# Per-token reciprocal roots: turned into rows on TensorE before they are written to device memory

## The chip, the core and the metric

The kernel runs on one core of a Trainium2 chip. The core has TensorE (PE, matrix products; PEld is its loading of weights), VectorE (DVE), ScalarE (ACT), GpSimd (POOL) and SyncE (SP). Here SP issues all transfers, in the order of one queue; 16 DMA engines carry them out. The metric is the device time of one execution in microseconds (us).

## What is computed

Two layers of a mixer over 2048 tokens of width 1024, in float32. Cut to what matters here:

```python
def rms_norm(x, g):
    y = xf * lax.rsqrt(jnp.mean(xf * xf, axis=-1, keepdims=True) + EPS)
    return y * g

for l in range(DEPTH):
    shift, scale, gate = jnp.split(c_act @ w_ada[l] + b_ada[l], 3, axis=-1)
    h = rms_norm(x, norm_g[l]) * (1.0 + scale) + shift
    proj = h @ w_in[l]                       # nine parts: q, k, v, gates of two groups of heads
    y = concatenate([gla_branch(...), diff_branch(...)]) @ w_out[l]
    x = x + gate * y
```

The change touches the `rsqrt(mean(x*x) + EPS)` of `rms_norm`: one number per token, by which a whole column of the transposed input is multiplied.

## The kernel before

The tokens are cut into units of 512 (`UT`), four per layer, so there are eight units, counted from 0 in each layer, with keys 0 to 7 (`key = l * NU + u`). Activations lie transposed: features on the 128 partitions, tokens along the free dimension. A unit goes through preparation (`prep_gen`: the normalised input `hhi`, `hlo`), nine projections (`dense_gen`, `out_gen`: matmuls into `acc` banks), a linear-attention group (`gla_gen`) and four heads of softmax attention (`qk_gen`, `attn_gen`). Each float32 factor is split into a high and a low part (`hi`, `lo`; `oh`, `ol`), so a product takes three matmuls.

The weights `w` don't fit into the on-chip memory. They come once as `raw`, are split, and are written back to device memory (`wd`, L958); later units read them from there (`w<-wd`, L579 to L594) into four buffers (`p_w`, L389). Matmuls that wait for weights wait for these reads.

The reciprocal roots of a unit take the following way. Their sums of squares come from two places: in the first layer, units 1 to 3, from ScalarE (`prep_gen`: tiles `xt` of 128 tokens, squares with a running sum into `xss`); in the second layer, from the output of the layer before (`out_gen`: squares of `rt` are added into `sqs`, and four matmuls with `ones` sum over the partitions, `sum_squares`, L633). Either way there is a tile of 128 partitions x 4: token 128 t + p stands in partition p, column t. `root` (L639) scales it on VectorE (`xms`) and raises it to the power -1/2 on GpSimd (`xrs`). What the preparation needs is a row of 512 numbers, the same in all 128 partitions (`rsb`). So `rs_write` (L649) writes the tile to device memory in the order of the tokens (`rd`), and `prep_gen` reads it back, spread over all partitions (`rsb<-rd`). In that write neighbours in memory come from different partitions: it consists of 512 pieces of 4 bytes. Seven of the eight units take this way; unit 0 of the first layer (`start`) makes `rsb` with four matmuls.

The order of the work is not the order of the source. All instructions are recorded (`Program.record`, L148; so every line in the profile is L375, and tiles tell the groups apart), streams of the parts are interleaved by a rough clock of PE (`run_streams`), and a planner (`best_order`, L218, and `order`, L251) lays out the instructions of every engine by estimated costs, 60 times with small changes of priority chosen by a fixed random seed, and keeps the best layout. It takes into account dependences, buffers and PSUM banks. Each engine then runs its list strictly in that order. For a transfer it reckons with the bytes divided by a rate that depends on the length of the last dimension, 350 bytes per ns where it is neither 64 nor 256; so the write `rd` has the same cost to it in pieces of 4 and of 512 bytes.

Of the kernel before, what the change touches and what calls it, by code (L numbers as in the profile page):

```python
# [12 lines left out]
F32 = mybir.dt.float32  # L13
# [4 lines left out]
ALU = mybir.AluOpType  # L18
# [4 lines left out]
P = 128  # L23
# [3 lines left out]
TT = UT // P  # L27
# [351 lines left out]
def trunk_kernel(ctx, tc, xl, x, c, ccol, w_ada, w_mod, w_all, w_glr, w_gk, vecs, lam, out):  # L379
    nc = tc.nc  # L380
    L = w_all.shape[0]
    NU = xl.shape[0]
# [13 lines left out]
    cst = pool("cst", 1)  # L396
    p_t = pool("p_t", 3)
    p_sm = pool("p_sm", 4)
# [5 lines left out]
    V, A, G, T, SY = (prog.queue(e) for e in "VAGTS")  # L404
# [7 lines left out]
    def tp():  # L412
        return ps_t.tile([P, 512], F32, tag="tp", name="tp")
# [8 lines left out]
    ident = cst.tile([P, P], F32, name="ident")  # L422
# [5 lines left out]
    mhalf = cst.tile([P, 16], F32, name="mhalf")  # L428
# [99 lines left out]
    def done(*ev):  # L528
        events[ev] = clock[0]
# [103 lines left out]
    def sum_squares(sqs):  # L633
        ps = sc()
        for t in range(TT):
            T.matmul(ps[:, 2 * t:2 * t + 1], sqs[:, t * P:(t + 1) * P], ones[:, 0:1], start=True, stop=True)
        return ps[:, 0:2 * TT].rearrange("p (t o) -> p t o", o=2)[:, :, 0]

    def root(ss):  # L639
        ms = p_sm.tile([P, TT], F32, tag="xms", name="xms", bufs=2)  # L640
        V.tensor_scalar(ms, ss, 1.0 / D, EPS, op0=ALU.mult, op1=ALU.add)
        rs = p_sm.tile([P, TT], F32, tag="xrs", name="xrs", bufs=2)
        G.tensor_tensor(rs, ms, mhalf[:, 0:TT], op=ALU.pow)
        return rs

    def rs_tile():
        return p_x.tile([P, UT], F32, tag="rsb", name="rsb", bufs=2)

    def rs_write(key, rs):  # L649
        SY.dma_start(RD[key].rearrange("o (t p) -> p (o t)", p=P), rs)  # L650

    def prep_gen(l, u, xsrc):
        key = l * NU + u
        if l == 0:
            yield need("h", key - 1, lag=6.0)
            ss = p_sm.tile([P, TT], F32, tag="xss", name="xss", bufs=2)
            for t in range(TT):
                xt = p_q.tile([P, D], F32, tag="q", name="xt")
                SY.dma_start(xt, x[u * UT + t * P:u * UT + (t + 1) * P, :])
                A.activation(xt, xt, AF.Square, accum_out=ss[:, t:t + 1])  # L660
                yield pe(0, 2.0)
            rs_write(key, root(ss))
        rsb = rs_tile()
        SY.dma_start(rsb, RD[key].broadcast_to([P, UT]))
        yield need("free_h", key)
        yield need("ada", l, 1)
        alloc_h()
        for c in range(KT // 2):
            xp = p_q.tile([P, 2, UT], F32, tag="q", name="xp")
            SY.dma_start(xp, xsrc(u)[:, 2 * c:2 * c + 2, :])  # L670
            for j in range(2):
                make_h(l, 2 * c + j, xp[:, j, :], rsb)
            yield pe(0.44, 1.2)
        done("h", key)

    def start():
        y = layers[0]
        SY.dma_start(vec, vecs)
        SY.dma_start(cact, ccol)
        cb = p_s.tile([P, D], F32, tag="s", name="cb")  # L680
        SY.dma_start(cb, c.broadcast_to([P, D]))
        xs = []
        sqs = p_x.tile([P, UT], F32, tag="sqs", name="sqs")

        def mod_load(k):
            wm = p_s.tile([P, 2, D], F32, tag="s", name="wm")
            SY.dma_start(wm, w_mod[k])
            return wm

        for c_ in range(KT // 2):  # L690
            xp = p_q.tile([P, 2, UT], F32, tag="q", name="xp")
            SY.dma_start(xp, src_in(0)[:, 2 * c_:2 * c_ + 2, :])
            xs.append(xp)
        th = p_s.tile([P, D], F32, tag="s", name="th0")
        A.activation(th, cb, AF.Tanh, scale=0.5)
        V.scalar_tensor_tensor(cb, th, 1.0, cb, op0=ALU.add, op1=ALU.mult)
        t8 = p_sm.tile([P, KT], F32, tag="t8", name="t8", bufs=1)
        A.activation(t8, cact, AF.Tanh, scale=0.5)
        V.scalar_tensor_tensor(cact, t8, 1.0, cact, op0=ALU.add, op1=ALU.mult)
        V.tensor_scalar(cact, cact, 0.5, None, op0=ALU.mult)  # L700
        wm = [mod_load(0)]
        for it in FIRST:
            early[it, 0] = load_raw(0, it, 0)
        wm.append(mod_load(1))
        for k in range(KT):
            add_square(sqs, xs[k // 2][:, k % 2, :], k == 0)
        rs = root(sum_squares(sqs))
        dg = t2()
        pb = tp()
        for t in range(TT):  # L710
            ts_ = slice(t * P, (t + 1) * P)
            V.tensor_scalar(dg[:, ts_], ident, rs[:, t:t + 1], None, op0=ALU.mult)
            T.matmul(pb[:, ts_], ones, dg[:, ts_], start=True, stop=True)
        rsb = rs_tile()
        A.copy(rsb, pb)
        y.A = cst.tile([P, KT], F32, name="A0")
        y.B = cst.tile([P, KT], F32, name="B0")
        alloc_h()
        for k in range(KT):
            if k % 2 and k + 1 < KT:  # L720
                for it in FIRST:
                    early[it, (k + 1) // 2] = load_raw(0, it, k + 1)
            if k + 2 < KT:
                wm.append(mod_load(k + 2))
            sv = p_sm.tile([P, 2], F32, tag="sv", name="sv", bufs=2)
            for part in range(2):
                V.scalar_tensor_tensor(wm[k][:, part, :], wm[k][:, part, :], 0.5, cb, op0=ALU.mult, op1=ALU.mult,
                                       accum_out=sv[:, part:part + 1])
            V.tensor_tensor(y.B[:, k:k + 1], sv[:, 0:1], vec[:, R_B + k:R_B + k + 1], op=ALU.add)
            V.scalar_tensor_tensor(sv[:, 1:2], sv[:, 1:2], 1.0, vec[:, R_B + 8 + k:R_B + 9 + k], op0=ALU.add, op1=ALU.add)  # L730
            V.tensor_tensor(y.A[:, k:k + 1], sv[:, 1:2], vec[:, R_N + k:R_N + k + 1], op=ALU.mult)
            make_h(0, k, xs[k // 2][:, k % 2, :], rsb)
            for it, ring in zip(FIRST, (acc, sc)):
                hi, lo = weights(0, 0, it, k)
                if k == 0:
                    first_banks[it] = [ring() for _ in range(4)]
                for j in range(4):
                    (mm3T if it >= 4 else mm3N)(first_banks[it][j], k, slice(j * P, (j + 1) * P), hi, lo)
        gate_weights(0)
        done("ada", 0, 1)  # L740
        done("h", 0)
# [219 lines left out]
    RD = [dram.tile([1, UT], F32, name=f"rd{k}") for k in range(L * NU)]  # L961
# [262 lines left out]
    def out_gen(l, u):  # L1224
        y = layers[l]
        key = l * NU + u
        xsrc, xdst = io(l)
        final = key == L * NU - 1
        if u == NU - 1:
            yield need("attn", key, 3)  # L1230
        if l < L - 1:
            sqs = p_x.tile([P, UT], F32, tag="sqs", name="sqs")
        for hf in range(2):
            ds = slice(4 * hf, 4 * hf + 4)
            banks = []
            for n_, k in enumerate((4, 5, 6, 0, 1, 2, 3, 7)):
                yield need("oT", key, 0 if k < 4 else k, lag=0.8)
                if n_ == 4:
                    rt = p_o.tile([P, 4, UT], F32, tag="osb", name="rt")
                    SY.dma_start(rt, xsrc(u)[:, ds, :])  # L1240
                hi, lo = weights(l, u, 7 + hf, k)
                oh, ol = oTs[key, k]
                for j in range(4):
                    js = slice(j * P, (j + 1) * P)
                    if n_ == 0:
                        banks.append(acc())
                    T.matmul(banks[j], hi[:, js], oh, start=(n_ == 0), stop=False)
                    T.matmul(banks[j], hi[:, js], ol, start=False, stop=False)
                    T.matmul(banks[j], lo[:, js], oh, start=False, stop=(n_ == KT - 1))
                    yield pe(0.65)  # L1250
            yield need("ada", l, 2)
            xo = xdst(u)[:, ds, :]
            for j in range(4):
                d = 4 * hf + j
                V.scalar_tensor_tensor(rt[:, j, :], banks[j], y.gate[:, d:d + 1], rt[:, j, :], op0=ALU.mult, op1=ALU.add)
                if final and hf == 1:
                    SY.dma_start(xo[:, j, :], rt[:, j, :])
                elif j % 2:
                    SY.dma_start(xo[:, j - 1:j + 1, :], rt[:, j - 1:j + 1, :])
                if l < L - 1:  # L1260
                    add_square(sqs, rt[:, j, :], d == 0)
        if l < L - 1:
            rs_write(key + NU, root(sum_squares(sqs)))
        done("x", key)

    def chain(*gens):
# [113 lines left out]
```

## Time and profile before

| | |
|---|---|
| median of 3 runs | 2469.76 us (2467.94 to 2473.55) |
| profiled execution | 2479.16 us, span 2477.2 us |
| mean granted TensorE clock | 0.99 |
| PE busy | 2388.0 us, 96% of the span |
| DVE, ACT, POOL busy | 74%, 50%, 5% |
| DMA | 573.77 MB, mean 232 GB/s |

A profile is one execution. Its views used below are: the page with busy times and the chain of work that ended last; the list of waits (who waited for whom: us in total, times, longest); groups of instructions (busy us, mean ns of one, idle time before); the timeline (start, duration, engine, tiles, and in brackets the idle time of the engine before and what ended it); stretches (busy us of each engine, then granted clock, DMA share, GB/s); and DMA issues (tiles, count, KB each, median us from issue to landing). An x after a name counts instructions. A row of the timeline that ends in x2 or more merges neighbours, so its duration runs to the end of the last.

### The profile page before, as it was taken

The numbers are of one execution on the slowest core, as the hardware profiler recorded it, in microseconds if no ns is written. First come the engines' busy times: TensorE is split into PE (matmuls) and PEld (weight loads), VectorE is DVE, ScalarE is ACT, GpSimd is POOL, SyncE is SP. The second block draws the span as 40 slices with busy tenths as digits, with TensorE's granted clock in tenths as the row PEclk, the third lists the DMA queues.
The fourth block names the chain that finished last, engine by engine and source line by source line (L and its number), as shares of the span: only waits on it lengthen the run. The fifth ranks groups of instructions, "written<-read, shape, count | busy, mean of one in ns | idle before, by whom it ended". The sixth has DMA issues, their size and how long they took to land.

```text
span 2477.2 us, 38561 instructions
## 1 busy us (share of the span) xinstructions
PE 2388.0 (96%) x12896; PEld 1944.8 (79%) x12896; DVE 1827.2 (74%) x5158; ACT 1240.6 (50%) x2726; POOL 123.2 (5%) x400
## 2 busy tenths in 40 slices
PE   6899899999999999899999999999999999999998
PEld 5687587887788878787788777888788887888787
DVE  8878676896568877388975797568863888737983
ACT  4776543555245553255674576245633555425542
POOL 0010000000000000000000000000000000000000
PEclk9899899999999999999999999999999999999999
DMA  7567898786967769675757886765686767876663
GB/s 297 188 252 257 264 307 260 242 260 217 246 210 226 241 209 270 184 221 178 237 197 242 288 283 221 263 230 178 227 277 211 242 207 234 247 229 197 198 209 119
DMA packets 373165, 573.77 MB, mean 232 GB/s; under 512 B 195492, under 2 KB 255336, under 8 KB 369896
## 3 DMA queue, kind: packets, MB, share of 16 engines
q1 hardware_dynamic: 372968, 571.32, 71.6%
q8 instruction: 102, 1.67, 0.3%
q14 instruction: 95, 0.78, 0.1%
HBM read 416.03 MB, written 161.50 MB: 233 GB/s over the span
## 4 chain that ended last, share of the span: by engine, by line
PE 71%; DVE 15%; DMA 7%; ACT 4%; issue 2%; SPq 1%; POOL 0%; POOLq 0%; DVEq 0%; ACTq 0%
PE acc L375 47%; PE sc L375 11%; PE po L375 9%; DVE s L375 6%; PE tp L375 4%; DMA wr<-in_w_ada_dram 3%; DMA w<-wd 2%; DVE t L375 1%; DVE w L375 1%; DVE am L375 1%; ACT s L375 1%; SPq L375 1%; ACT qh L375 1%; DMA s<-ad 1%; DVE hlo L375 1%
## 5 line engine op out<-in xcount | busy, mean ns | idle before, releaser
L375 PE MATMUL acc<-w,hhi 128*128 128x512 f32 x2560 | 832.6, 401 | 9.5 <-DVE t L375 2.6
L375 PEld LDWEIGHTS acc<-w,hhi 128*128 128x128 f32 x2560 | 468.4, 190 | 100.2 <-DVE t L375 4.9
L375 PE MATMUL acc<-w,hlo 128*128 128x512 f32 x1280 | 506.7, 397 | 0.0
L375 ACT ACTIVATE s<-s,mx 128x512 f32<-128x512 f32 (+15 forms) x256 | 308.3, 1204 | 308.8 <-DVE s L375 162.7
L375 PE MATMUL acc<-oh,w 128*128 128x512 f32 x1024 | 358.7, 402 | 6.7 <-DMA w<-wd 3.6
L375 DVE TENSOR_SCALAR_CACHE_REDUCE s<-sc,mx 64x64 f32<-64x64 f32 (+5 forms) x640 | 307.6, 483 | 49.9 <-PE sc L375 29.8
L375 PE MATMUL acc<-hhi,w 128*128 128x512 f32 x960 | 323.4, 402 | 10.7 <-DMA w<-wd 9.5
L375 PEld LDWEIGHTS acc<-w,hlo 128*128 128x128 f32 x1280 | 242.2, 189 | 49.9 <-issue 0.9
L375 PEld LDWEIGHTS acc<-oh,w 128*128 128x128 f32 x1024 | 193.0, 189 | 50.3 <-DMA w<-wd 4.0
L375 PEld LDWEIGHTS acc<-hhi,w 128*128 128x128 f32 x960 | 181.5, 190 | 49.7 <-DMA w<-wd 11.1
L375 PEld LDWEIGHTS po<-Vj,s 128*128 128x128 f32 x1536 | 194.8, 197 | 11.1 <-DMA s<-ad 4.2
L375 PE MATMUL po<-Vj,s 128*128 128x128 f32 x1536 | 199.8, 282 | 3.5 <-DMA s<-ad 2.0
L375 PE MATMUL acc<-ol,w 128*128 128x512 f32 x512 | 202.2, 395 | 0.0
L375 DVE SCALAR_TENSOR_TENSOR s<-s,r 128x512 f32<-128x512 f32 (+2 forms) x320 | 198.5, 667 | 2.4
L375 PE MATMUL acc<-hlo,w 128*128 128x512 f32 x480 | 190.4, 397 | 0.0
L375 DVE TENSOR_SCALAR_CACHE_REDUCE s<-sc 128x512 f32<-128x512 f32 (+4 forms) x256 | 158.2, 622 | 41.4 <-PE sc L375 33.3
L375 PE MATMUL sc<-Kj,qh 128*128 128x512 f32 x384 | 162.0, 422 | 4.4 <-DVE s L375 4.4
L375 ACT CAST w<-raw 128x512 fp32r<-128x512 f32 x160 | 97.7, 622 | 112.1 <-PE acc L375 83.6
L375 PE MATMUL sc<-Kj,ql 128*128 128x512 f32 x384 | 152.2, 396 | 0.0
L375 DVE TENSOR_TENSOR w<-raw,w 128x512 fp32r<-128x512 f32 x160 | 108.9, 686 | 53.5 <-ACT w L375 52.7
L375 DVE SCALAR_TENSOR_TENSOR t<-ub,vec,t 128x512 f32<-128x512 f32 x192 | 138.3, 747 | 5.6 <-ACT t L375 5.1
L375 POOL MEMSET s<- 64x64 f32 x256 | 37.0, 145 | 2102.5 <-PE po L375 1522.7
(181 smaller groups left out, 3581.0 us busy)
## 6 DMA issues: line engine op xcount, KB each, us to landing
w<-wd SPq DMA_DIRECT2D x416, 512.0 KB, 4.5
wd<-w SPq DMA_DIRECT2D x144, 512.0 KB, 4.8
raw<-in_w_all_dram SPq DMA_DIRECT2D x80, 512.0 KB, 6.7
Kj<-kd SPq DMA_DIRECT2D x48, 512.0 KB, 5.5
ad<-s SPq DMA_DIRECT2D x24, 768.0 KB, 4.9
s<-ad SPq DMA_DIRECT2D x24, 768.0 KB, 6.7
wr<-in_w_ada_dram SPq DMA_DIRECT2D x128, 128.0 KB, 3.9
ad<-s SPq DMA_DIRECT2D x32, 512.0 KB, 4.1
```

Of the source, the lines that this page charges most:

```text
L375: getattr(self.engines[e], method)(*[real(a) for a in args], **{k: real(v) for k, v in kw.items()})
```

## The change

`root` now writes into the first four columns of a fixed tile of 128 x 128 (`rs128`, cleared once at the start). `rs_write` calls `root`, transposes the whole tile on PE into a PSUM bank, copies the first four rows to a tile `xrr` of 4 partitions x 128 on VectorE, and writes that: four rows of 128 consecutive tokens, so four pieces of 512 bytes. For unit 0 only the name of the tile changes.

```diff
+    rs128 = cst.tile([P, P], F32, name="rs128")
+    V.memset(rs128, 0.0)
+
     def root(ss):
         ms = p_sm.tile([P, TT], F32, tag="xms", name="xms", bufs=2)
         V.tensor_scalar(ms, ss, 1.0 / D, EPS, op0=ALU.mult, op1=ALU.add)
-        rs = p_sm.tile([P, TT], F32, tag="xrs", name="xrs", bufs=2)
-        G.tensor_tensor(rs, ms, mhalf[:, 0:TT], op=ALU.pow)
-        return rs
+        G.tensor_tensor(rs128[:, 0:TT], ms, mhalf[:, 0:TT], op=ALU.pow)
...
-    def rs_write(key, rs):
-        SY.dma_start(RD[key].rearrange("o (t p) -> p (o t)", p=P), rs)
+    def rs_write(key, ss):
+        root(ss)
+        ps = tp()
+        T.transpose(ps[:, 0:P], rs128, ident)
+        rr = p_sm.tile([TT, P], F32, tag="xrr", name="xrr", bufs=1)
+        V.tensor_copy(rr, ps[0:TT, 0:P])
+        SY.dma_start(RD[key].rearrange("o (t p) -> (o t) p", p=P), rr)
...
-            rs_write(key, root(ss))
+            rs_write(key, ss)
...
-        rs = root(sum_squares(sqs))
+        root(sum_squares(sqs))
...
-            V.tensor_scalar(dg[:, ts_], ident, rs[:, t:t + 1], None, op0=ALU.mult)
+            V.tensor_scalar(dg[:, ts_], ident, rs128[:, t:t + 1], None, op0=ALU.mult)
...
-            rs_write(key + NU, root(sum_squares(sqs)))
+            rs_write(key + NU, sum_squares(sqs))
```

PE has seven more instructions, VectorE eight; SP, ACT and POOL have as many as before. Since the planner lays out everything anew, neighbours change places all over the program. Three places matter below.

SP's queue at the roots of unit 3 of the first layer (in the trace near 587 us), before and now; `rd` is the write, `rsb<-rd` the read of it, `w<-wd` are weights, `vd`, `vp` and `Vj` values of the attention:

```order
L375 DMA Vj<-vp_1_1191 128x512
L375 DMA rd_6443<-xrs 128x4x1
L375 DMA vd_0_6497<-Vt 128x512
L375 DMA rsb<-rd_6443 128x512
L375 DMA w<-wd_7_1_3322 128x1024
L375 DMA w<-wd_7_2_3358 128x1024
L375 DMA vp_0_6543<-vd_0_6497 128x1x512
L375 DMA w<-wd_7_3_3448 128x1024
```

```order
L375 DMA Vj<-vp_1_1162 128x512
L375 DMA rd_6491<-xrr 4x128
L375 DMA vd_0_6510<-Vt 128x512
L375 DMA w<-wd_7_1_3324 128x1024
L375 DMA rsb<-rd_6491 128x512
L375 DMA w<-wd_7_2_3353 128x1024
L375 DMA vp_0_6556<-vd_0_6510 128x1x512
L375 DMA w<-wd_7_3_3427 128x1024
```

The write stands where it stood. One load of weights that stood behind the read `rsb<-rd` now stands ahead of it.

SP's queue at the roots of unit 2 of the second layer (near 988 us), before and now; `xd` is the residual stream, `ad` probabilities of the attention:

```order
L375 DMA s<-ad_3_10146 128x24x64
L375 DMA Vj<-vp_1_1191 128x512
L375 DMA rd_10223<-xrs 128x4x1
L375 DMA w<-wd_4_4_3985 128x1024
L375 DMA w<-wd_4_5_3992 128x1024
L375 DMA xd_9854<-rt 128x1024
L375 DMA w<-wd_4_6_4026 128x1024
L375 DMA Vj<-vp_1_4429 128x512
L375 DMA Vj<-vp_1_7504 128x512
L375 DMA w<-wd_4_7_4034 128x1024
```

```order
L375 DMA Vj<-vp_1_1162 128x512
L375 DMA w<-wd_4_4_3996 128x1024
L375 DMA rd_10249<-xrr 4x128
L375 DMA w<-wd_4_5_4018 128x1024
L375 DMA xd_9870<-rt 128x1024
L375 DMA w<-wd_4_6_4043 128x1024
L375 DMA Vj<-vp_1_4439 128x512
L375 DMA Vj<-vp_1_7520 128x512
L375 DMA w<-wd_4_7_4063 128x1024
```

One load of weights went from behind the write to ahead of it; three stand within the next six rows, as before.

PE's list at the same unit, from the sums of squares (`sc<-ones,sqs`) on, before and now:

```order
L375 MATMUL sc<-ones,sqs 128x1 x4
L375 MATMUL po<-Vt,s 128x128 x4
L375 MATMUL acc<-hhi,w 128x512
L375 MATMUL acc<-hlo,w 128x512
L375 MATMUL acc<-hhi,w 128x512 x2
L375 MATMUL acc<-hlo,w 128x512
L375 MATMUL acc<-hhi,w 128x512 x2
```

```order
L375 MATMUL sc<-ones,sqs 128x1 x4
L375 MATMUL po<-Vt,s 128x128 x4
L375 MATMUL acc<-hhi,w 128x512
L375 MATMUL acc<-hlo,w 128x512
L375 MATMUL acc<-hhi,w 128x512 x2
L375 MATMUL tp<-ident,rs_115 128x128
L375 MATMUL acc<-hlo,w 128x512
L375 MATMUL acc<-hhi,w 128x512 x2
```

The transpose stands eight matmuls behind the sums: four short ones of the attention (`po`) and four of the projection (`acc`).

## Prediction

> **What bounds the kernel now.** I read the page first: the engines' busy times and the chain that ended last.
>
> ```profile
> span 2477.2 us, 38561 instructions
> ...
> PE 2388.0 (96%) x12896; PEld 1944.8 (79%) x12896; DVE 1827.2 (74%) x5158; ACT 1240.6 (50%) x2726; POOL 123.2 (5%) x400
> ...
> PE 71%; DVE 15%; DMA 7%; ACT 4%; issue 2%; SPq 1%; POOL 0%; POOLq 0%; DVEq 0%; ACTq 0%
> ```
>
> TensorE (PE) is busy for 2388.0 of 2477.2 us. A change that takes no matmul away can therefore win only out of the 89.2 us in which PE idles, and out of stretches in which its granted clock is below full. So the next view is who PE waited for, and the one after it is PE's timeline at the longest of these waits.
>
> ```profile
> PE acc L375 <- DMA w<-wd: 15.5, 5, 6.2
> PE sc L375 <- DVE sqs L375: 14.7, 1, 14.7
> ```
>
> ```profile
> 385.98 0.70 PE L375 MATMUL acc<-w,hhi 128*128 128x512 f32 x2 [2.40 <-DMA w<-wd]
> 603.00 0.50 PE L375 MATMUL acc<-oh,w 128*128 128x512 f32 x1 [3.58 <-DMA w<-wd]
> 674.09 0.50 PE L375 MATMUL acc<-hhi,w 128*128 128x512 f32 x1 [2.95 <-DMA w<-wd]
> 1001.01 0.80 PE L375 MATMUL acc<-hhi,w 128*128 128x512 f32 x1 [6.22 <-DMA w<-wd]
> ```
>
> The wait for `sqs` is the start of the program and stays. The largest other item is the wait for weights `w` read back from device memory: 15.5 us, of which these four make 2.40 + 3.58 + 2.95 + 6.22 = 15.15. What stood in the DMA queue ahead of each? The timeline of SyncE (SP), the only queue that issues transfers, answers:
>
> ```profile
> 363.61 1.36 SPq L375 DMA_DIRECT2D rd<-xrs  x1
> ...
> 586.85 0.37 SPq L375 DMA_DIRECT2D rd<-xrs  x1
> 590.38 0.32 SPq L375 DMA_DIRECT2D vd<-Vt  x1
> 595.68 0.32 SPq L375 DMA_DIRECT2D rsb<-rd  x1
> 596.10 0.86 SPq L375 DMA_DIRECT2D w<-wd  x2
> ...
> 659.74 0.37 SPq L375 DMA_DIRECT2D rd<-xrs  x1
> ...
> 988.06 0.39 SPq L375 DMA_DIRECT2D rd<-xrs  x1
> 988.54 0.93 SPq L375 DMA_DIRECT2D w<-wd  x2
> ```
>
> Each of the four waits ends 13 to 22 us after a write `rd<-xrs`, which is the write that the change rewrites. The DMA issues tell how odd this write is: it has 2 KB and lands later than 512 KB of weights.
>
> ```profile
> w<-wd SPq DMA_DIRECT2D x416, 512.0 KB, 4.5
> ...
> wd<-w SPq DMA_DIRECT2D x144, 512.0 KB, 4.8
> ...
> wr<-in_w_ada_dram SPq DMA_DIRECT2D x128, 128.0 KB, 3.9
> ...
> rd<-xrs SPq DMA_DIRECT2D x7, 2.0 KB, 11.5
> ```
>
> Last I read stretches of 6 to 8 us behind four of the writes, and a normal stretch of the same kind. The last three columns are granted clock, busy share of the DMA engines, and GB/s.
>
> ```profile
> 368.00:374.00 6.00, 5.18 (x23) 3.98 (x23) 1.39 (x2) 1.24 (x2) 0.00 (x0) 1.00 1.25 114
> 662.00:670.00 8.00, 8.00 (x38) 6.58 (x38) 1.10 (x2) 1.35 (x4) 0.69 (x2) 1.00 1.08 72
> 990.00:998.00 8.00, 4.79 (x33) 4.10 (x31) 0.35 (x1) 0.66 (x3) 0.69 (x2) 1.00 1.14 57
> 1358.00:1366.00 8.00, 8.00 (x37) 6.61 (x36) 1.37 (x2) 1.25 (x2) 0.00 (x0) 1.00 1.13 99
> 1366.00:1374.00 8.00, 8.00 (x38) 6.42 (x36) 5.37 (x12) 5.79 (x10) 0.00 (x0) 1.00 0.97 364
> ```
>
> Behind a write of 512 pieces the DMA engines are shown as fully busy, and they move 57 to 114 GB/s instead of 364. The large transfers issued next crawl for some 8 us. That is the mechanism on which the prediction rests.
>
> **The change part by part.** *The write itself.* The two weight loads to look at are the one issued at 988.54 and the one at 664.56; asked for singly, they show
>
> ```profile
> w<-wd SPq DMA_DIRECT2D x1, 512.0 KB, 12.4
> ```
>
> ```profile
> w<-wd SPq DMA_DIRECT2D x1, 512.0 KB, 9.5
> ```
>
> 988.54 + 12.4 is 1000.9 and 664.56 + 9.5 is 674.1: the moments at which PE starts again. With the usual 4.5 they would be there at 993.0 and 669.1. PE stopped at 1001.01 − 6.22 = 994.8 and 674.09 − 2.95 = 671.1, so both waits go. At 603.00 the way is another one: the read `rsb<-rd` has to wait until the write has landed, and holds SP from 590.7 to 595.68 with the weight loads behind it. PE stopped at 599.4. In the new order one weight load stands ahead of that read; it leaves at about 590.8 and is there at 595.3. At 385.98 it was SP that came late. Its waits between 370 and 381 are led by
>
> ```profile
> SPq L375 <- DMA wr<-in_w_ada_dram: 5.5, 1, 5.5
> ```
>
> a load of 128 KB that fell into the stretch of 114 GB/s; with it SP was held 5.5 us, more than PE's 2.40. So 15.15 us of waiting can go.
>
> *The clock.* Behind three of these waits the granted clock fell:
>
> ```profile
> 602.00:608.00 6.00, 5.00 (x15) 3.96 (x16) 2.84 (x6) 0.00 (x0) 0.00 (x0) 0.72 0.88 356
> 674.00:680.00 6.00, 5.59 (x16) 4.20 (x17) 0.00 (x0) 0.00 (x0) 0.00 (x0) 0.72 0.40 162
> 1001.00:1007.00 6.00, 5.99 (x15) 4.58 (x16) 0.75 (x1) 0.69 (x1) 0.00 (x0) 0.52 0.84 339
> ```
>
> 6 us at 0.72 lose 1.7 us of PE's work, twice, and 6 us at 0.52 lose 2.9: together 6.3 us. The gain is at most 15.15 + 6.3 = 21.4 us.
>
> *What comes back at once.* Where the weights no longer end the wait, the vector engines may. Behind 990 VectorE (DVE) is busy 0.35 and ScalarE (ACT) 0.66 of 8 us, behind 662 DVE 1.10: both have time to spare. Behind 586 they haven't:
>
> ```profile
> 588.00:596.00 8.00, 8.00 (x39) 6.39 (x38) 6.45 (x26) 2.84 (x11) 0.15 (x1) 1.00 0.13 38
> ```
>
> DVE is busy 6.45 of 8 us there. I count this place as given back whole, 3.58 + 1.7 = 5.3 us, so 16.1 us remain. That is my choice; it may be 0.
>
> *What is added.* On PE seven transposes, on DVE seven copies out of PSUM and one fill at the start. The nearest rows:
>
> ```profile
> L375 PE MATMUL tp<-ident,rw 128*128 128x128 f32 x256 | 42.9, 276 | 3.2 <-DVE rw L375 3.0
> ...
> L375 DVE COPY a_sb<-tp 128x8 f32<-128x8 f32 x16 | 1.9, 157 | 1.6 <-PE tp L375 1.6
> ```
>
> A transpose takes 276 ns alone and 42.9 / 256 = 0.17 us among others, so 1.2 to 1.9 us on the engine that sets the end; I take 1.9, since each stands alone. The copies, 7 x 157 ns = 1.1 us, lie beside matmuls, as DVE has a quarter of the span free; uncovered they would cost that 1.1.
>
> *The new wait.* PE runs its queue in order. Now a transpose stands in it that needs the root from GpSimd (POOL), and behind it stand the matmuls of the projections. How long the root takes shows at 657:
>
> ```profile
> 657.84 0.58 PE L375 MATMUL sc<-ones,sqs 128*128 128x1 f32 x4
> 658.46 0.16 DVE L375 TENSOR_SCALAR xms<-sc 128x4 f32<-128x4 f32 x1
> 658.71 1.01 POOL L375 TENSOR_TENSOR xrs<-xms,mhalf 128x4 f32<-128x4 f32 x1 [0.55 <-DVE xms L375]
> ```
>
> From the end of the sums on PE (658.42) to the end of the root (659.72) it is 1.30 us. In the new order eight matmuls lie between at the unit quoted in the section on the change, four of 8.00 / 38 = 0.21 us (the stretch from 662) and four short ones. I take the short ones at the 0.17 of a transpose: 1.5 us in all. The root is just hidden. At the four places of this kind I take 0.15 us each, 0.6 in all. At the other three the root hangs on ACT's squares of the loaded `xt`:
>
> ```profile
> 108.94 0.17 DVE L375 TENSOR_SCALAR xms<-xss 128x4 f32<-128x4 f32 x1 [0.62 <-ACT xt L375]
> ...
> ACT s L375 <- DVE s L375: 163.2, 102, 8.4
> ```
>
> DVE waited 0.62 us for those there; I take 0.6 for PE each time, 1.8 in all. The far bound is the longest single wait of ACT for DVE, 8.4 us each. Below nothing the wait can't be. SP now waits for the copy instead of the root, some 0.8 us later (0.276 + 0.157 and hand-offs); behind it stand weight loads. At 988.54 these have 994.8 − 993.0 = 1.8 us to spare, so it costs nothing there; without that cover it would cost the 0.8.
>
> *The order.* The planner redraws the order of the whole program, and on PE it differs in many small places. I take 0 for it, and a bound of 3 us either way: that is a fifth of the 15.5 us which the longest group of waits in the trace makes.
>
> *The sum.* −21.4 + 5.3 + 1.9 + 0.6 + 1.8 = −11.8 us. The profiled execution took 2479.16 us, of which its span is 2477.2; the median of the runs is 2469.76, 9.4 us less. I subtract the sum from both: 2467.4 for a profiled execution, and **2458 us** for the median. That the unprofiled runs have the same waits is an assumption.
>
> *A rule and the rows.* The new write is not in the trace. Its nearest rows are the load of 128 KB, 3.9 us, and the old write, 11.5 us. I take the lower, as it has 4 pieces and the old one 512; with the upper one and the crawl behind it the sum would be the first rival's. The Trainium skill, page "DMA: Bandwidth & Descriptors", section "Specifications", names 512 bytes as the least size of a transfer at full rate, below which the DMA engine reads, changes and writes back. By this rule the new write just escapes, and the sum is the −11.8 above. The trace agrees that 4 bytes are far too little (11.5 us for 2 KB), and no run here shows where the border lies.
>
> **The rivals.** *First: the pieces are not what is slow.* It could be the write into device memory itself, or what else runs in those moments. Then the landing stays at 11.5, the queue crawls as before, the four waits stay, and only the costs come: 1.9 + 0.6 + 1.8 = 4.3 us at most, 2474, nearer to 2472 if the holds stay hidden. In this case the change does not do what it says. For it speaks that only runs with such writes are at hand. Against it speak four slow stretches behind four such writes, while weight writes to the same memory land in 4.8 us. The Trainium skill gives this rival a ground: on the same page, section "Anatomy of one DMA — SWDGE (gpsimd) path", it says of another way of issuing that a transfer's fixed cost is mostly the receipt of the write, and "This can cause a surprisingly long delay especially when the write target is HBM." The trace shows long landings of this write, and not which of the two it is.
>
> *Second: the waits go, and PE finds the next one.* PE may meet attention's vector work earlier at more places than 603. If two thirds of the 21.4 come back, the sum is −7.1 + 4.3 = −2.8, 2467. For it: DVE 74% busy and 15% of the chain. Against it: DVE and ACT stand nearly idle behind 662 and 990.
>
> *Third, slower: PE is held at the transposes of the first layer.* In the three units whose root hangs on ACT, PE reaches the transpose with the root not there. Everything behind it waits, projections included. With the bound of 8.4 us each and a half-clock stretch of 1.7 behind each, this is 3 x 10.1 = 30.3 us against 16.1 − 1.9 − 0.6 = 13.6 of gain: 16.7 us slower, 2486. It decides for slower by over 0.2% from a hold of 13.6 + 4.9 = 18.5 us in all. Against it: ACT is busy for half the span only, and DVE waited just 0.62 us there.
>
> **How the numbers follow.** 0.2% is 4.9 us, about what a measurement of this kernel can tell from no change; so faster means under 2464.8 and slower over 2474.7. The forecast has 0.68 (0.63 faster, 0.05 same), its own range 2446 to 2466: the low end is −21.4 + 1.2 − 3 = −23.2 us. The first rival has 0.10 (0.07 same, 0.03 slower), the second 0.14 (0.07 faster, 0.06 same, 0.01 slower), the third 0.08 (0.01 same, 0.07 slower). Together: faster 0.70, same 0.19, slower 0.11. The range runs from 2446 to 2473 and takes in most of the first two rivals.
>
> **What would show it.** Right: `rd` lands within about 4 us, the stretches behind it move over 300 GB/s, PE's waits for `w` fall from 15.5 us to under 5, and no half-clock stretch stands near 603, 674 and 1001. The holds show as PE's waits at `tp<-ident,rs`, 2.4 us in all. Wrong: `rd` still lands after 8 us or more; or waits for `w` are gone while PE's idle time is as long, now ended by DVE or ACT; or single holds at the transposes of over 5 us.

## The result and the profile after

| | before | after |
|---|---|---|
| median | 2469.02 us (4 runs) | 2447.16 us (4 runs, 2444.97 to 2448.36) |
| profiled execution | 2479.16 us, span 2477.2 | 2444.97 us, span 2443.3 |

The ratio is 0.9907, with a 95% interval of 0.989 to 0.9924: faster by 21.9 us. The forecast was −11.8 us, so the direction was right and the size short by nearly half. The two profiles lie further apart than the medians (34.2 us), because the profiled execution of before was 9.4 us above its median; a second profile of it, below, took 2467.67 us.

The page of the changed kernel, its span, busy times and chain:

```profile
span 2443.3 us, 38591 instructions
...
PE 2375.5 (97%) x12903; PEld 1941.1 (79%) x12903; DVE 1828.8 (75%) x5166; ACT 1240.2 (51%) x2726; POOL 124.3 (5%) x400
...
PE 75%; DVE 13%; DMA 5%; ACT 4%; issue 2%; POOL 0%; SPq 0%; POOLq 0%; DVEq 0%; ACTq 0%
```

PE idles for 67.8 us instead of 89.2, and its busy time is 12.5 us shorter in spite of seven more matmuls (8.5 us against the second profile of before, 2384.0): fewer of them ran at a reduced clock. The list of waits shows what became of the 15.5 us:

```profile
PE sc L375 <- DVE sqs L375: 14.6, 1, 14.6
PE sc L375 <- DVE s L375: 8.7, 10, 1.7
...
PE acc L375 <- DMA w<-wd: 0.3, 1, 0.3
```

PE's waiting for weights has gone, and no DMA stands among its larger waits. Had the write itself become fast? Its landing is not recorded in this trace, but the read of it tells. It waits for the write to land, and the timeline of SP's queue at the first unit shows when it leaves:

```profile
111.68 0.27 SPq L375 DMA_DIRECT2D rd<-xrr  x1
...
113.31 0.38 SPq L375 DMA_DIRECT2D rsb<-rd  x1
```

Write and read lie 1.63 us apart, so the write landed within that time; before, a write took 11.5 us to land. The stretches behind three of the writes (357.0, 644.9 and 967.4 us); the last columns are clock, DMA share and GB/s:

```profile
361.00:367.00 6.00, 6.00 (x32) 5.06 (x31) 2.14 (x5) 2.17 (x6) 0.69 (x2) 1.00 0.93 374
648.00:656.00 8.00, 8.00 (x39) 6.60 (x38) 0.75 (x1) 0.69 (x1) 0.00 (x0) 1.00 0.39 137
970.00:978.00 8.00, 8.00 (x49) 7.07 (x48) 0.35 (x1) 1.35 (x4) 0.69 (x2) 1.00 0.99 355
```

Where much is asked of the DMA engines they move 355 to 374 GB/s; the 137 stands beside a share of 0.39, so little was asked there. Before, shares of 1.08 to 1.25 went with 57 to 114. PE is busy without a gap in all three. Last, the group of what was added, and the idle time of the engines ahead of its instructions:

```profile
L375 PE MATMUL tp<-ident,rs x7: 270/272/473, 110.6 to 1327.9; 128*128 128x128 f32 x7
...
  POOL rs L375: 0.7, 3
```

A transpose takes 272 ns (minimum, median and maximum stand before the times), and an engine of the group waited for the root three times, 0.7 us in all. PE's matmuls are not among them: twice it was the weight loading of a transpose (PEld), 0.4 us in all, and once DVE at unit 0, which waited as long in the kernel before.

### The profile page after: what moved, and what is told of

It reads as the page before. It is cut to its first block, busy times and chain, and to the rows that moved or that the text cites. A ratio compares the mean times of both kernels' runs of the same rounds, so it can differ in the third digit from the quotient of the medians.

```text
span 2443.3 us, 38591 instructions
## 1 busy us (share of the span) xinstructions
PE 2375.5 (97%) x12903; PEld 1941.1 (79%) x12903; DVE 1828.8 (75%) x5166; ACT 1240.2 (51%) x2726; POOL 124.3 (5%) x400
## 4 chain that ended last, share of the span: by engine, by line
PE 75%; DVE 13%; DMA 5%; ACT 4%; issue 2%; POOL 0%; SPq 0%; POOLq 0%; DVEq 0%; ACTq 0%
PE acc L375 50%; PE sc L375 11%; PE po L375 9%; DVE s L375 6%; PE tp L375 4%; DMA wr<-in_w_ada_dram 2%; DVE t L375 1%; ACT s L375 1%; DVE w L375 1%; DMA xt<-in_x_dram 1%; ACT qh L375 1%; DVE am L375 0%; ACT t L375 0%; DVE r L375 0%; DMA xp<-xd 0%
```

## The experiments

The theory: 512 pieces of 4 bytes keep the DMA engines busy for some 10 us, and what is queued behind the write crawls, whoever waits for it. The first rival: the late landing of the write is what costs (its reader holds SP). The second: it is the new order of the program that pays. In all kernels an edit is put in where the recorded instructions are issued, behind the planner, unless it is said otherwise, so that it moves nothing else. A ratio is taken to executions of the kernel before that belong to the same series; their median was 2469.02 us in one series and 2471.24 in another, so times of different series can be compared to some 2 us only.

**The kernel before, once more** (`e0_before_again`, nothing edited).

> The kernel before, unchanged, for a second profile of it. The pieces theory (512 pieces of 4 bytes clog the DMA queue for some 8 us and the weight loads behind them come late) expects the same picture: PE waits for w of 10 to 16 us, all within 25 us of a write rd, and time 2465 to 2474 us. If the four waits of the first profile were an accident of that execution, their sum is under 5 us here.

Measured: 2467.79 us, ratio 0.9991 (0.9979 to 1.0004). PE's waits for weights in this second profile, the group and the single ones:

```profile
PE acc L375 <- DMA w<-wd: 10.7, 5, 5.4
```

```profile
384.55 0.70 PE L375 MATMUL acc<-w,hhi 128*128 128x512 f32 x2 [1.19 <-DMA w<-wd]
598.85 0.50 PE L375 MATMUL acc<-oh,w 128*128 128x512 f32 x1 [2.66 <-DMA w<-wd]
668.22 0.50 PE L375 MATMUL acc<-hhi,w 128*128 128x512 f32 x1 [1.24 <-DMA w<-wd]
...
992.55 0.79 PE L375 MATMUL acc<-hhi,w 128*128 128x512 f32 x1 [5.38 <-DMA w<-wd]
```

The places are the four of the prediction, so they belong to the kernel. Their sizes do not: 15.5 us in the first profile, 10.7 in this one.

**The new order with the old pieces** (`e1_after_order_512`). Transposes and copies stay, in their places; the write takes the column tile again, in 512 pieces.

```diff
+            args = self.swap.get(i, args)
...
+        prog.swap[len(prog.ops)] = (RD[key].rearrange("o (t p) -> p (o t)", p=P), rs128[:, 0:TT])
         SY.dma_start(RD[key].rearrange("o (t p) -> (o t) p", p=P), rr)
```

> The changed kernel in its own order of instructions, transposes and copies included; only the write goes out of the root's tile again in 512 pieces of 4 bytes. Pieces theory: the gain goes, 2462 to 2474 us, PE waits for w again 8 us or more. Order theory (the new layout of the program is what gained): the gain stays, 2445 to 2452 us, no waits for w.

Measured: 2464.48 us, ratio 0.997 (0.9958 to 0.9982).

```profile
PE acc L377 <- DMA w<-wd: 7.3, 4, 2.6
```

With the old pieces two thirds of the gain are lost, and PE's waits for weights are back, at 7.3 us a little under the 8 expected. The order is worth something of its own, some 7 us with the costs of the transposes in it. The wait near 600 us is missing here: the weight load that the new order put ahead of the read leaves at 586.56 us, while the read is held until 589.94; in the second profile of before the read left at 591.67 and that load behind it. Whether this explains the 7 us was not tried by itself.

**The old order with the new write** (`e2_before_order_turned`). Before, with each write replaced, where it stands, by transpose, copy and a write of four pieces.

```diff
+        def turned(eng, dst, src):
+            ps = ps_t.pool.tile([P, 512], F32, tag="tp", name="tp")
+            eng["T"].transpose(ps[0:TT, 0:P], src, ident.real())
+            rr = p_sm.pool.tile([TT, P], F32, tag="xrr", name="xrr", bufs=1)
+            eng["V"].tensor_copy(rr, ps[0:TT, 0:P])
+            eng["S"].dma_start(RD[key].real().rearrange("o (t p) -> (o t) p", p=P), rr)
+        prog.turn[len(prog.ops)] = turned
```

> The order of the kernel before, kept for all its instructions; each write rd is replaced, where it stands, by a transpose, a copy and a write in 4 pieces of 512 bytes. Pieces theory: 2444 to 2454 us, no waits for w near the writes. Order theory: 2462 to 2474 us.

Measured: 2449.56 us, ratio 0.991 (0.9896 to 0.9923), PE's waits for weights 0.3 us. The write alone makes the whole gain; the second rival falls. The two effects do not add: the order pays 7 us only while the old pieces are there.

The two kernels of the same order can be laid side by side. Below are four stretches of before (second profile) that begin near a write, and then the stretches of this experiment with the same matmuls:

```profile
279.20:366.40 87.20, 83.08 (x402) 67.28 (x402) 63.33 (x171) 42.93 (x94) 4.18 (x11) 0.98 0.90 309
584.50:668.20 83.70, 79.82 (x401) 65.98 (x399) 52.29 (x143) 30.03 (x66) 5.19 (x14) 0.98 0.82 234
963.60:1052.90 89.30, 83.92 (x402) 69.71 (x401) 39.90 (x98) 26.02 (x57) 2.76 (x8) 0.96 0.71 204
1334.80:1484.50 149.70, 145.94 (x802) 116.10 (x801) 117.82 (x330) 87.00 (x205) 7.24 (x23) 1.00 0.81 275
```

```profile
282.20:363.90 81.70, 80.82 (x403) 66.14 (x403) 63.98 (x171) 42.68 (x93) 4.17 (x11) 1.00 0.92 323
582.00:659.70 77.70, 77.70 (x402) 65.16 (x401) 52.47 (x144) 29.65 (x63) 4.76 (x13) 1.00 0.79 252
954.50:1035.80 81.30, 81.30 (x403) 67.77 (x402) 40.48 (x100) 26.03 (x57) 3.08 (x8) 1.00 0.69 223
1317.60:1463.60 146.00, 144.71 (x803) 116.28 (x802) 118.15 (x331) 87.32 (x205) 7.24 (x23) 1.00 0.79 282
```

The second number of a row is its length: 5.5, 6.0, 8.0 and 3.7 us shorter, 23.2 in all, more than the 16.4 by which the two spans differ. The clock is enough for the rest. Read in stretches of 5 us, one minus the granted clock adds up to 6.8 us in before within these four stretches and to nothing in the experiment, but elsewhere to 13.6 us in before and 22.2 in the experiment. Those other losses lie before 130 us, near 260 and, in the experiment, near 2410; they differ from one execution to the next. Two of the places, the first and the last, hardly show among the waits for `w`. At the first, the waits of DVE and PE between 282 and 306 us of before say why:

```profile
DVE am L375 <- DMA wr<-in_w_ada_dram: 11.1, 4, 5.7
...
PE tp L375 <- DVE rw L375: 2.4, 1, 2.4
...
PE acc L375 <- DVE z L375: 0.9, 1, 0.9
```

and in the same part of the experiment

```profile
DVE am L379 <- DMA wr<-in_w_ada_dram: 3.9, 2, 3.2
```

Other loads, of 128 KB, crawl too. DVE stands before them 11.1 us instead of 3.9, what is queued behind on DVE comes late, and PE's wait appears under the name of DVE. PE's two lines have no counterpart in the experiment. At the last place ACT waits 7.4 us for transfers `wd<-w` in before and 0.6 us in the experiment.

**One old write kept** (`e7_key3_old`): the experiment before, with the 512 pieces left at unit 3 of the first layer, the place near 600 us.

```diff
-        prog.turn[len(prog.ops)] = turned
+        if key != 3:
+            prog.turn[len(prog.ops)] = turned
```

> The order of the kernel before with the transposed write at six of the seven places; at unit 3 of the first layer (the wait that ended at 603 us) the old write in 512 pieces stays. The prediction counted this place as given back whole to VectorE: then this is as fast as with all seven, 2447 to 2452 us. If nothing is given back there, it is slower by the wait and the half clock behind it, 4 to 6 us: 2453 to 2457 us.

Measured: 2452.96 us, ratio 0.9925 (0.9901 to 0.9948), 3.4 us more than with all seven turned, at the lower edge of the 4 to 6 us expected. The two intervals overlap, so the time alone does not decide; the trace carries the verdict:

```profile
595.55 0.50 PE L379 MATMUL acc<-oh,w 128*128 128x512 f32 x1 [2.32 <-DMA w<-wd]
```

```profile
585.00:593.00 8.00, 8.00 (x40) 6.40 (x38) 5.36 (x19) 3.06 (x5) 0.00 (x0) 1.00 0.38 64
```

The wait is back where the old write is. With all seven turned PE is busy 79.39 of the 80 us from 560 on, here 77.29: the 2.1 us that go with the wait are not taken back by DVE or ACT. The half clock did not come with it: from 596 to 602 us the granted clock is 1.00.

**A write that nobody reads** (`e3_unread_512x4`). The changed kernel, plus behind each write a second one of 512 pieces of 4 bytes, into memory that nothing reads; no instruction waits for it.

```diff
+        def again(eng):
+            extra = dram.pool.tile([1, UT], F32, name=f"rx{key}")
+            r = rs128.real()
+            eng["S"].dma_start(extra.rearrange("o (t p) -> p (o t)", p=P), r[:, 0:TT])
+        prog.more[len(prog.ops)] = again
```

> The changed kernel, and behind each of its seven writes one more write of the same 2 KB in 512 pieces of 4 bytes to memory that nobody reads and nobody waits for. Pieces theory: the queue clogs as before, 2458 to 2474 us, PE waits for w of 8 us or more. Landing theory (what cost time was that the read of the roots had to wait for a late landing): 2445 to 2451 us, as nothing waits for this write.

Measured: 2472.06 us, ratio 0.9998 (0.9987 to 1.001). The waits, and two stretches behind such writes:

```profile
PE acc L376 <- DMA w<-wd: 14.9, 7, 5.2
```

```profile
662.00:670.00 8.00, 7.54 (x36) 5.88 (x34) 0.89 (x2) 0.69 (x1) 0.00 (x0) 1.00 0.96 32
994.00:1002.00 8.00, 4.71 (x33) 4.01 (x31) 0.35 (x1) 0.66 (x3) 0.68 (x2) 1.00 1.22 94
```

The whole gain is lost, 22.5 us by the two ratios and 24.9 by the medians of two series, to 14 KB that nobody asked for. PE's largest waits stand near 600, 673 and 1004 us again. The rival of the late landing falls: the roots' own write is as fast here as in the changed kernel. At unit 3 its read leaves 3.57 us behind it, against 3.56 there, and SP waits for no `rd`. What costs is the DMA engines behind the pieces, at shares of 0.96 and 1.22 with 32 and 94 GB/s.

**What in the pieces is slow?** Six more kernels change only the shape of the unread write: the count of its pieces, their size, or what lies beside them.

Every piece in a 512-byte block of its own (`e4_unread_512x4_apart`):

```diff
+            extra = dram.pool.tile([UT, P], F32, name=f"rx{key}")
+            eng["S"].dma_start(extra.rearrange("(t p) c -> p t c", p=P)[:, :, 0:1], r[:, 0:TT].rearrange("p (t o) -> p t o", o=1))
```

> As the run with the unread second write of 512 pieces of 4 bytes, but each piece goes to a block of 512 bytes of its own. If many small pieces are slow because neighbouring ones fall into the same block of memory and have to wait for each other, this costs little: 2446 to 2453 us, no waits for w. If small pieces are slow wherever they go: 2458 to 2476 us, waits for w of 8 us or more. I expect the first with 0.6.

512 pieces of 512 bytes, 256 KB (`e5_unread_512x512`):

```diff
+            extra = dram.pool.tile([P, TT, 2, P], F32, name=f"rx{key}")
+            eng["S"].dma_start(extra[:, :, 0, :], r.unsqueeze(1).to_broadcast([P, TT, P]))
```

> The changed kernel, and behind each write one more unread write of 512 pieces, each of 512 bytes (256 KB in all). If the number of pieces is what clogs the queue: 2458 us or more. If their size is: the extra 7 x 256 KB are some 0.6 us of DMA time each, 2446 to 2452 us, waits for w under 4 us.

128 pieces of 16 bytes without gaps (`e6_unread_128x16`):

```diff
+            extra = dram.pool.tile([P, TT], F32, name=f"rx{key}")
+            eng["S"].dma_start(extra, r[:, 0:TT])
```

> The changed kernel, and behind each write one more unread write of the same 2 KB in 128 pieces of 16 bytes, one from each partition. If each small piece costs its time: a quarter of the 25 us that 512 pieces cost, 2450 to 2456 us. If what counts is how many pieces share a block of memory (32 here, 128 before), about the same. If nothing shows (2446 to 2449 us), the clog needs more pieces than 128.

512 pieces of 4 bytes at steps of 8, neighbours from different partitions (`e8_unread_step8_mixed`), and with the four of a partition side by side (`e9_unread_step8_own`):

```diff
+            extra = dram.pool.tile([UT, 2], F32, name=f"rx{key}")
+            eng["S"].dma_start(extra.rearrange("(t p) c -> p t c", p=P)[:, :, 0:1], r[:, 0:TT].rearrange("p (t o) -> p t o", o=1))
```

> The changed kernel with an unread second write of 512 pieces of 4 bytes, every 8 bytes one (64 in a block of 512 bytes, neighbours from different partitions); the dense write had 128 in a block and cost 25 us, one in a block cost 2. If the cost grows with the pieces that share a block: 8 to 18 us over the changed kernel, 2455 to 2466 us. If only pieces that touch each other without a gap are slow: 2447 to 2451 us.

```diff
+            eng["S"].dma_start(extra.rearrange("(p t) c -> p t c", p=P)[:, :, 0:1], r[:, 0:TT].rearrange("p (t o) -> p t o", o=1))
```

> The same 512 pieces every 8 bytes, but the four of a partition side by side, so that a short stretch of memory gets its pieces from few partitions. If pieces sharing a block are slow whoever sends them: as in the run with mixed neighbours. If the clog comes from neighbours that different DMA engines write: under half of that run's loss, at best 2447 to 2451 us.

128 pieces of 4 bytes without gaps, one block of 512 bytes (`e10_unread_128x4`):

```diff
+            extra = dram.pool.tile([P, 1], F32, name=f"rx{key}")
+            eng["S"].dma_start(extra, r[:, 0:1])
```

> The changed kernel with an unread second write of 128 pieces of 4 bytes, one from each partition, dense, filling one block of 512 bytes. If each dense piece costs the same: a quarter of 25 us, 2451 to 2456 us. If a clog needs more pieces: 2446 to 2450 us.

| unread write | median us | ratio to before (95%) | PE's waits for `w`, us |
|---|---|---|---|
| none: the changed kernel | 2447.16 | 0.9907 (0.989 to 0.9924) | 0.3 |
| 512 x 4 B, no gaps (e3) | 2472.06 | 0.9998 (0.9987 to 1.001) | 14.9 |
| 128 x 4 B, no gaps (e10) | 2462.48 | 0.9965 (0.995 to 0.998) | 6.7 |
| 512 x 4 B, own blocks (e4) | 2449.37 | 0.9911 (0.9883 to 0.9939) | 0.9 |
| 512 x 4 B, steps of 8, mixed (e8) | 2449.29 | 0.9909 (0.9885 to 0.9934) | none |
| 512 x 4 B, steps of 8, own (e9) | 2448.84 | 0.9906 (0.9877 to 0.9935) | none |
| 128 x 16 B, no gaps (e6) | 2449.01 | 0.9909 (0.9885 to 0.9932) | 0.4 |
| 512 x 512 B (e5) | 2449.49 | 0.9911 (0.9888 to 0.9934) | none |

The landings of the unread writes, the last number of each row, in the order e3, e10, e4, e8, e6:

```profile
rx<-rs SPq DMA_DIRECT2D x7, 2.0 KB, 11.1
```

```profile
rx<-rs SPq DMA_DIRECT2D x7, 0.5 KB, 8.6
```

```profile
rx<-rs SPq DMA_DIRECT2D x7, 2.0 KB, 2.1
```

```profile
rx<-rs SPq DMA_DIRECT2D x7, 2.0 KB, 4.6
```

```profile
rx<-rs SPq DMA_DIRECT2D x7, 2.0 KB, 2.8
```

Neither the number of pieces (e4, e5) nor their smallness by itself (e4, e6, e8, e9) costs anything that these runs can tell. Nor were gap-free pieces sent as another number of packets: the traces of e3, e4, e5, e8 and e9 all count 373222 packets, those of e6 and e10 both 370534. The 4-byte pieces cost when they lie next to each other without a gap, and then a quarter of them already costs 14.3 us by the ratios. That is outside both of the ranges expected for e10, and it answers the question left by e6: 128 pieces are enough. My idea that the cost grows with the number of pieces in one block of 512 bytes fell with e10 and with e8, whose pieces share blocks too. Why pieces without gaps are slow stays open. The gaps of e8 also halve the pieces in any smaller block, so these runs do not separate the missing gap from a full block; 4-byte pieces in gap-free pairs only, or a gap-free run from one partition, were not tried.

**The same cure without PE** (`e11_packed_rows`). Before, in which each partition writes its four roots as one piece of 16 bytes. The row comes back in another order, so that the multiplication on DVE reads it with a step of four elements. Here the planner works anew; the order of PE, DVE and ACT came out as in before.

```diff
+        x3 = xk.rearrange("p (t q) -> p t q", t=TT)
+        r3 = rsb.rearrange("p (q t) -> p t q", t=TT) if packed else rsb.rearrange("p (t q) -> p t q", t=TT)
-        V.scalar_tensor_tensor(xk, xk, y.A[:, k:k + 1], rsb, op0=ALU.mult, op1=ALU.mult)
+        V.scalar_tensor_tensor(x3, x3, y.A[:, k:k + 1], r3, op0=ALU.mult, op1=ALU.mult)
...
-        SY.dma_start(RD[key].rearrange("o (t p) -> p (o t)", p=P), rs)
+        SY.dma_start(RD[key].rearrange("o (p t) -> p (o t)", p=P), rs)
```

> A version without TensorE: the order of the kernel before, the roots written as they lie, 16 bytes from each partition (128 pieces), read back as a row and used with a step of four elements in the multiplication that prepares the input. If 128 pieces of 16 bytes are harmless, as the unread write of that kind was, the gain is there without transposes and their waits: 2443 to 2449 us. If the stepped reading slows VectorE's 64 multiplications (0.75 us each) by half, that is 24 us of VectorE beside matmuls, 2447 to 2460 us.

Measured: 2467.41 us, ratio 0.9987 (0.9975 to 1.0). PE's waits for weights are 0.2 us, so the crawl is gone here too, and yet next to nothing is won: the time lies above both ranges that were expected. The group of that multiplication, here and then with the old order and the new write (e2); the two numbers behind the bar are busy us and mean ns:

```profile
L375 DVE SCALAR_TENSOR_TENSOR xp<-xp,A,rsb 128x512 f32<-128x512 f32 x64 | 68.6, 1094 | 2.9 <-DMA xp<-xd 1.5 <-DMA xp<-in_xl_dram 1.2
```

```profile
L379 DVE SCALAR_TENSOR_TENSOR xp<-xp,A,rsb 128x512 f32<-128x512 f32 x64 | 46.3, 745 | 4.4 <-DMA xp<-xd 3.0 <-DMA xp<-in_xl_dram 1.2
```

The step costs DVE 22.3 us in multiplications that the projections wait for, and the kernel is 17.9 us above e2. That the one makes the other is argued from these sizes and the equal order; it was not tried by itself. No version beat the changed kernel.

## Why the prediction was right and its size wrong

*The mechanism* holds. The pieces make what is queued behind them crawl (e3 restores all of it with a write for which nobody waits), and PE's waits at the four places come from this (e2, and e7 for one of them). The first rival, with the pieces not slow, falls by e2; the second, with PE finding the next wait, by the stretches in which PE is now busy without a gap; the third by the holds of at most 0.4 us where it needed 18.5.

*The gain, 21.4 us.* The direct waits went from 15.5 to 0.3, and at 602, 674 and 1001 us the clock after is 1.00. But the term was read from an execution 9.4 us above its median. In the second profile, which lies at the median, the four waits make 10.5 us instead of 15.15. The clock loses 6.8 us there instead of the 6.3, but at other places: 1.7 us near 305, 1.7 near 600 and 3.4 near 995, and nothing behind the wait at 668; in e2 and in the changed kernel nothing is lost at these places. On the other side the term left out waits under other names. By the second profile these are 2.4 for `rw` and 0.9 for `z` near 300, and 1.2 for `w` of DVE and 0.5 for `ub` of ACT near 1370: 5.0 us. So 22.3 us: nearly the 21.4, but by luck, as 4.7 us too much and 5.0 left out cancel.

*What comes back at once.* This is the step that failed: "I count this place as given back whole, 3.58 + 1.7 = 5.3 us". Nothing comes back: in the changed kernel PE waits for nothing between 580 and 600 us, and e7 shows that the old write at this place alone costs its 2.3 us of waiting. The reason given, DVE busy 6.45 of 8 us, was no reason. In the changed kernel, 16 us behind the same write, DVE is busier still, 7.28 of 8 us, and PE is busy throughout:

```profile
594.00:602.00 8.00, 8.00 (x39) 6.71 (x38) 7.28 (x24) 4.11 (x6) 0.00 (x0) 1.00 0.53 173
```

How busy an engine is does not say that PE needs its work then.

*The costs.* Seven transposes of 272 ns are the 1.9 us that were taken; each is shown to start before the matmul ahead of it ends, so this is the most that they cost. The copies take 279 ns instead of 157 and lie beside matmuls, as assumed. The holds were put at 2.4 us and are at most 0.4.

*The order*, taken as 0 with a bound of 3: the changed kernel and e2, which differ in the order, have ratios of 0.9907 and 0.991. Right, but only for the new write; with the old one the order is worth 7 us.

*The sum* with what was measured, −22.3 + 1.9 + 0.4 = −20.0, stands against −21.9. Of the missing 10.1 us, 5.3 are what did not come back, 2.0 the holds and 0.9 the gain; the last 1.9 I could not split: the interval of the ratio alone runs from 19 to 27 us.

*The chances* were added up wrongly: the rows make 0.71 for faster and 0.18 for the same, not 0.70 and 0.19.

*The rule on small transfers.* The changed kernel had the outcome that the Trainium skill's page "DMA: Bandwidth & Descriptors", section "Specifications", led to expect. The rule there, that a transfer under 512 bytes is read, changed and written back, does not tell the cases apart: by it, e4, e6, e8 and e9 would have to pay as well, and they land in 2.1 to 4.6 us and cost nothing that shows. The measurement decides: among the shapes tried in this kernel the border is not at a size of piece but between 4-byte pieces with and without a gap. The long receipt of a write, of which the same page of the Trainium skill speaks in its section "Anatomy of one DMA — SWDGE (gpsimd) path", is not what was paid here: in e3 no one waits for the receipt.

## What to carry to other kernels

Cost a transfer by what stands behind it in the queue, not by its bytes or by who waits for it: 2 KB at seven places cost 22 us. Count the waits behind such a cause by place, over the stretch that follows, since they turn up under the names of other engines. Count nothing as given back because an engine is busy there; ask whether the waiting engine needs that work then.

## What was not expected of the hardware

Gap-free 4-byte writes to device memory hold up the DMA engines, and the same pieces with gaps of 4 bytes do not: landings of 11.1 against 4.6 us, and 22 to 25 us of the kernel's time against at most 2.1, which lies within the intervals. A second operand with a step of 16 bytes takes DVE's multiplication of 128 x 512 numbers from 745 to 1094 ns in the mean, with the eight of the first unit, which have no step, in it.
